# An encoder block on one core: values products of a head moved back, selection rounds spread, and one weight of a short pair summed on chip

## The chip, the cores and the metric

The kernel runs on one core of a Trainium2 chip. A core has TensorE (matmuls, PE in the profile; its weight loads are PEld), VectorE (DVE), ScalarE (ACT), GpSimd (POOL) and SyncE (SP, which here only issues DMAs). Each engine works through its own queue in order; semaphores tie the queues together. The metric is the device time of one execution in microseconds: 1687.0 us, the median of three runs (1686.08 to 1688.25).

## The reference, cut to what matters

One layer of a streaming encoder on 512 frames of width 2048, all in float32:

```
h = rmsnorm(x)
aq, ak, av, az, iq, ik, iw, rq, rk, rv, rz, ga, gb = split(h @ w_in)
index  = sum over 16 heads of relu(iq . ik) * iw           # which keys a query may use
sel    = the top 128 keys of each query, within its chunks
a_out  = softmax(aq . ak * scale + bias, over sel) @ av * silu(az)      # 8 heads of 128
b_out  = groupnorm(retention(rope(rq), rope(rk), rv)) * silu(rz)        # 8 heads of 128
merged = sigmoid(ga) * (a_out @ w_a_out) + sigmoid(gb) * (b_out @ w_b_out)
r = x + merged @ w_o
y = rmsnorm(r + (p @ w_ple) * sigmoid(r @ w_ple_gate))
```

Nearly all of the arithmetic is matrix products of 512 frames with weights that are read once. Three places matter here: the product of a head's probabilities with its values (`@ av`), the selection of the top keys, and the product `b_out @ w_b_out`.

## The kernel before

**Weights in two parts.** TensorE multiplies a weight block as a high part (float32r) and a low part, the rest. A *unit* is one weight block of up to eight 128x128 tiles. For each unit SyncE loads a raw tile (`wraw`, line 150), ScalarE writes the high part `wh` (line 176), VectorE subtracts it from the raw tile and so writes the low part `wl` (line 183). Raw tiles have 7 slots, `wh` and `wl` 3 each. Splitting runs `AHEAD` = 3 units before use (`reach`), loading `LOADS` = 5 units before that (`load_reach`).

**Pairs.** Two output blocks are computed together from seven products instead of eight (`gemm_pair`). The seven weights are sums of the four blocks b11, b12, b21, b22 (`block_pair`): the first is b12 + b22, the second b11, then b21 and b22; the fifth is the first + b11, the sixth the fifth + b21, and the seventh b11 + b12. In the order of the code's tuples the raw tile `t` is used for the first, fifth and sixth, and `w11` for the second and the seventh. b12 + b22 is made by a DMA that accumulates onto the loaded tile (`add_block`, line 137, issued by GpSimd). So are the fifth weight (b11 onto `t`, once the first weight has been split) and the seventh (b12 onto `w11`, once the second has been split). Only b21 is added by VectorE (line 185), as that tile is on chip anyway. The sums of the frames that go with the seven products are made earlier. In a pair, the products go to four PSUM banks p, v, q, r; after some of them ScalarE copies a bank (`pv`, `e`, line 279) and VectorE takes differences (`e_t`, line 283). The bank p is used by the second, fifth and seventh product, and the next of these on it waits for the copy.

**Short pairs.** Most pairs have blocks of eight tiles. The four pairs of `b_out @ w_b_out` (`project_two`, for m = 6, 8, 10, 12) have blocks of four. Two raw tiles, two `wh` or two `wl` of such units share one slot (`shared`). While such units are near, loads run up to `HALF_LOADS` = 14 units ahead, and the accumulation that makes b12 + b22 is issued 16 steps after its load. The differences of a short pair are added by GpSimd (line 1276), two by two: after the third and the sixth product one addition each, after the seventh two.

**Steps.** The order of all side work is written out in steps. `step()` is called after every two matmuls of a pair (56 steps in a pair, 28 in a short one) or every three of a plain product; `later(n, f)` puts f into the queues n steps on. What is put there stands in each engine's queue at that place and runs when the engine reaches it and its semaphores allow.

**Heads.** Attention head h is spread over three pairs (`attention_head`): its query and key product is the pair itself; logits, softmax and transposes of the probabilities (`ps_pt`) run beside the next pair; ScalarE's high part `pth` and VectorE's low part `ptl` (line 1143) at the turn to the pair after; then the values products (`outs`, line 1157), at 69, 69, 73, 73 steps after the head's own pair, which is at steps 13 and 17 of a pair of 56. The product of the third matmul uses the low part of the second block, the sixth that of the third. The gate (line 1170) runs on GpSimd at 77, the store at 92. The logits of the next head come at steps 20, 22, 24 and 26 of the same pair. PSUM has 8 banks, of which the pair holds four.

**Selection.** The top keys are found in 16 rounds for each of three tiles of queries, each a `MAX8` and a `MATCH_REPLACE8` on VectorE (lines 767, 768). Rounds are background work: `step` takes one from a list when the step number is a multiple of the current rate. In the four `rz` pairs and the three `az` pairs that follow (from 774.8 to 923.9 us) the rate is `BG_RATES[5]` = 9. The list has to be empty after them; the mask is then stored, and added to the bias tile of each head by a DMA 8 steps before the end of its own pair (line 1072).

Of the kernel before, what the change touches and what calls it, by code (L numbers as in the profile page):

```python
# [34 lines left out]
def block_kernel(tc, xT, pT, posb, posq, w_in, w_v, w_k, w_a, w_b, w_o, w_ple, w_gate,  # L35
                 w_gt, w_pt, fgb, tab, xg, cst, dec, out, out_a, out_b):
    nc = tc.nc
    pe, dve, act, pool, sp = nc.tensor, nc.vector, nc.scalar, nc.gpsimd, nc.sync

    with contextlib.ExitStack() as ctx:  # L40
# [10 lines left out]
        def U(name, dt=F32):  # L51
            return up.tile([128, L], dt, name=name, tag="u")

        def B(name, dt=F32):
            return bp.tile([128, 1280], dt, name=name, tag="b")

        def P(name):
            return pp.tile([128, L], F32, name=name, tag="p")
# [11 lines left out]
        raw_tiles = {}  # L70
# [5 lines left out]
        def raw(src, k0, nk, cols, plus=None):  # L76
            raws.append((src, k0, nk, cols, plus))
            return len(raws) - 1
# [9 lines left out]
        def block_pair(s1, s2, nk=8):  # L88

            b11, b12, b21, b22 = (s1, 0), (s2, 0), (s1, nk), (s2, nk)
            first = len(units)
            t = raw(*b12, nk, 128, b22)
            w11, w21, w22 = (raw(*b, nk, 128) for b in (b11, b21, b22))
            for r, plus in ((t, b11), (w11, b12), (w21, None), (w22, None), (t, w21), (t, None), (w11, None)):
                units.append((r, plus, nk, 128))
            if nk < 8:
                half_raws.update((t, w11, w21, w22))
                half_units.update(range(first, first + 7))  # L100
            return list(range(first, first + 7))

        half_raws, half_units = set(), set()
        open_tiles = {}

        def shared(kind, dt, tag, bufs=None):
            t = open_tiles.pop(kind, None)
            if t is not None:
                return t[:, 4:8, :]
            more = {} if bufs is None else {"bufs": bufs}  # L110
            t = open_tiles[kind] = wp.tile([128, 8, 128], dt, name=tag, tag=tag, **more)
            return t[:, 0:4, :]

        def load_reach(i):
            n = i + AHEAD + LOADS
            if any(i + d in half_units for d in range(AHEAD)):
                n = max(n, min(i + HALF_LOADS, max(half_units) + 3))
            return n
# [13 lines left out]
        def view(t, nk, cols):  # L132
            return t.rearrange("p a c -> p (a c)")[:, 0:nk * cols].rearrange("p (a c) -> p a c", c=cols)

        def add_block(r, b):
            src, k0 = b
            pool.dma_start(out=raw_tiles[r], in_=src[:, k0:k0 + raws[r][2], :], accum_op=OP.add)  # L137

        def load_to(n):
            need = max((u[0] for u in units[:n]), default=-1) + 1  # L140
            while state["raw"] < need:
                i = state["raw"]
                src, k0, nk, cols, plus = raws[i]
                if nk * cols <= L and i < 4:
                    t = U("wraw4").rearrange("p (a c) -> p a c", c=128)
                elif i in half_raws:
                    t = shared("raw", F32, "wraw", RAW_BUFS)
                else:
                    t = wp.tile([128, 8, 128], F32, name="wraw", tag="wraw", bufs=RAW_BUFS)
                sp.dma_start(view(t, nk, cols), src[:, k0:k0 + nk, :])  # L150
                raw_tiles[i] = t
                if plus is not None:
                    later(16 if i in half_raws else 0, lambda i=i, plus=plus: add_block(i, plus))
                state["raw"] += 1

        def split_to(n):
            while state["split"] < min(n, len(units)):
                i = state["split"]
                load_to(i + 1)
                r, plus, nk, cols = units[i]  # L160
                if r in unfinished:
                    unfinished[r]()
                raw = view(raw_tiles[r], nk, cols)
                if i in half_units:
                    h, l = (shared(n, F32R, n) for n in ("wh", "wl"))
                elif i in in_raws:
                    t = wp.tile([128, 2, 512], F32R, name="whl", tag="wraw", bufs=RAW_BUFS)
                    h, l = t[:, 0:1], t[:, 1:2]
                elif nk * cols == L:
                    h, l = (U(n, F32R).rearrange("p (a c) -> p a c", c=cols) for n in ("wh4", "wl4"))  # L170
                else:
                    h, l = (view(wp.tile([128, 8, 128], F32R, name=n, tag=n), nk, cols) for n in ("wh", "wl"))
                if i == 0:
                    dve.tensor_copy(h, raw)  # L174
                else:
                    act.activation(h, raw, AF.Copy)  # L176

                def rest(i=i, r=r, plus=plus, l=l, raw=raw, h=h, nk=nk, cols=cols):
                    if i in finished:
                        return  # L180
                    finished.add(i)
                    unfinished.pop(r)
                    dve.tensor_sub(l, raw, h.bitcast(F32))  # L183
                    if isinstance(plus, int):
                        dve.tensor_add(raw, raw, view(raw_tiles[plus], nk, cols))  # L185
                    elif plus is not None:
                        add_block(r, plus)

                unfinished[r] = rest
                later(1 if i else 0, rest)  # L190
                loaded[i] = (h, l)
                state["split"] += 1
# [7 lines left out]
        def later(n, f):  # L200
            if n <= 0:
                return f()
            tick[1] += 1
            heapq.heappush(soon, (tick[0] + n, tick[1], f))
# [234 lines left out]
        for k in range(KT):  # L439
# [7 lines left out]
            elif k < 10:  # L447
                t = U("xk")
                sp.dma_start(t, xT[:, k, :])
                xs.append(t)  # L450
            elif k % 2 == 0:
                t = B("xk2")
# [277 lines left out]
        def values_store(c0, pss):  # L730
            for t, ps in enumerate(pss):
                n = ps.shape[1]
                v = U("rv")[:, 0:n]
                act.activation(v, ps, AF.Copy, scale=R["nat"][:, t:t + 1])
                act.dma_start(rd[t, :, c0:c0 + n], v)
# [8 lines left out]
        for n, f in ((50, f_pos), (54, lambda: f_table(0)), (59, lambda: f_table(1))):  # L744
            later(n, f)
        state["rate"] = BG_RATES[0]
        values_store(0, values(u_rv[0], 512, late=2))
        state["rate"] = BG_RATES[1]
        pss = values(u_rv[1], 296)
        f_keys0(pss)  # L750
        todo.extend([None] * 4 + [f_keys1] + [None] * 10 + [f_keys2] + N3 * 4 + [f_keys3] + N3 * 2)
        state["rate"] = BG_RATES[2]
        ix = [iq_split(gemm(u_iq[m], hparts, "ps_iq", slice(128, L))) for m in range(IQ_PLAIN)]
# [7 lines left out]

        state["rate"] = BG_RATES[1]

# [224 lines left out]
        assert not bg, len(bg)  # L988
        state["rate"] = BG_RATES[3]
        for m in range(IQ_PLAIN):  # L990
# [37 lines left out]
        for kind, n, u in pairs:  # L1028
# [9 lines left out]
            else:  # L1038
# [4 lines left out]
                elif n == G_FIRST:  # L1043
                    state["rate"] = BG_RATES[4]
                gate_pair(u, to(d[m:m + 2], AF.Sigmoid))
# [16 lines left out]
        def attention_head(h):  # L1062
# [85 lines left out]
            def outs(n):  # L1148
                if n == 0:
                    E["po"] = P("ps_o")  # L1150
                po = E["po"]
                for i in range(3 * n, min(3 * n + 3, len(seq))):
                    a, b, j = seq[i]
                    if j == NT - 1:
                        pe.matmul(po[:, 384:], E["v"][0][:, tok(3)].bitcast(F32), E["p3"][:, 0:128], start=False, stop=False)
                    else:
                        pe.matmul(po[:, 128 * j:], E["v"][a][:, tok(j)], E["p"][b][:, JOFF[j]:JOFF[j] + L - 128 * j],
                                  start=(i == 0), stop=(i == len(seq) - 1))
                if n == 3:
                    E["oT"] = U("oT")  # L1160
                    act.activation(E["oT"], po, AF.Copy)
# [13 lines left out]
            steps = [(-30, loads), (-8, mask), (30, values_load)]  # L1175
# [2 lines left out]
            steps += [(54, lambda i=i: turn(i)) for i in range(3)]  # L1178
            steps += [(n, lambda i=i: high(i)) for i, n in enumerate((56, 56, 58))]
            steps += [(n, lambda i=i: low(i)) for i, n in enumerate((58, 58, 60))]  # L1180
            steps += [(n, lambda i=i: outs(i)) for i, n in enumerate((69, 69, 73, 73))]
            steps += [(48, z_load), (77, gate), (92, store)]
            return done, steps

        for n in range(Z_FIRST):
# [2 lines left out]
        for h in range(NH):  # L1188
            done, steps = attention_head(h)
# [110 lines left out]
        for m in PAIRED:  # L1300
            t = B("sm")
# [97 lines left out]
        for m in range(MF):  # L1399
            i = u_p[m // 4][0]  # L1400
# [12 lines left out]
            if m < Y_APART or m >= Y_APART + 2:  # L1413
                t = U("pw")
            else:
                if m == Y_APART:
                    ypair[m // 2] = B("y2")
                t = ypair[m // 2][:, L * (m % 2):L * (m % 2) + L]
# [44 lines left out]
        for n in range(MF // 2):  # L1463
            t = B("go")
            outs = t[:, 0:512], t[:, 512:1024]
# [156 lines left out]
AHEAD = 3  # L1622
LOADS = 5
BG_RATE = 4
BG_RATES = (3, 3, 4, 10, 8, 9)
IQ_PLAIN = 2
G_FIRST = 2
X_STAY = 3
# [3 lines left out]
ROUNDS_FIRST = 0  # L1632
PAIR_STEPS = 56
B_PAIRS = 6
HALF_LOADS = 14
Z_FIRST = 3
ROUND_GAP = 11
STORE_LAG = 16
# [97 lines left out]
```

## Time and profile before

| | |
|---|---|
| runs, median (lowest to highest) | 1687.0 us (1686.08 to 1688.25) |
| profiled execution | 1688.58 us |
| its span, first to last instruction | 1686.8 us |
| granted TensorE clock, mean | 0.995 |
| TensorE matmul busy | 1654.5 us, 98% |
| VectorE busy | 1420.1 us, 84% |
| ScalarE busy | 963.2 us, 57% |
| GpSimd busy | 352.7 us, 21% |
| mean DMA rate | 227 GB/s |

How to read it: a row of the timeline gives start, length, engine, source line and operation, output and inputs; in brackets the idle time of the engine before it and what ended that. A row of the waits says who waited for whom, the total in us, how often, and the longest. A row of the stage windows gives the window, its length, the busy time of PE, PEld, DVE, ACT and POOL, the granted clock as a share of the full one, the DMA share and GB/s. The ends of matmuls are modelled; their starts are not.

### The profile page before, as it was taken

What the parts mean: (1) busy time and instruction counts of PE and PEld (TensorE: products, weight loads), DVE (VectorE), ACT (ScalarE), POOL (GpSimd) and SP (SyncE); (2) the same over time, 40 slices, a digit from 0 to 9 for tenths busy, and PEclk for the clock granted to TensorE, in tenths of its full rate; (3) what the DMA queues carried; (4) which work ended last, traced back from release to release, by engine and by line L of the source; (5) the groups of instructions that cost most, each with busy time, mean ns of one, the idle gap of its engine ahead of it and who ended that gap; (6) DMA issues with size and microseconds to landing.
All of it is one profiled execution on the core that took longest, in us unless ns stands there. A gap on an engine that the chain in (4) does not pass through costs nothing.

```text
span 1686.8 us, 26584 instructions
## 1 busy us (share of the span) xinstructions
PE 1654.5 (98%) x9632; PEld 1457.4 (86%) x9632; DVE 1420.1 (84%) x2257; ACT 963.2 (57%) x1501; POOL 352.7 (21%) x355
## 2 busy tenths in 40 slices
PE   9999999999999999999999999999899999999998
PEld 7999998888888888888888877878788888888897
DVE  8789887888889889889997777678788888899895
ACT  6557666555555555555545656557443454487673
POOL 3011111111111111111554112124330033311211
PEclk9999999999999999999999999999999999999999
DMA  8779888887888888877879998875987699999873
GB/s 305 255 238 253 206 209 198 207 205 198 216 208 212 210 206 214 221 199 209 245 197 232 255 239 206 235 178 207 276 301 222 161 251 287 260 322 238 214 243 125
DMA packets 144163, 382.19 MB, mean 227 GB/s; under 512 B 15648, under 2 KB 30112, under 8 KB 144032
## 3 DMA queue, kind: packets, MB, share of 16 engines
q1 hardware_dynamic: 106528, 261.20, 44.5%
q0 software_dynamic: 29872, 106.44, 35.2%
q10 hardware_dynamic: 7632, 12.85, 2.2%
q8 instruction: 76, 1.25, 0.3%
q14 instruction: 55, 0.45, 0.1%
HBM read 331.28 MB, written 49.15 MB: 226 GB/s over the span
## 4 chain that ended last, share of the span: by engine, by line
PE 79%; DVE 8%; ACT 4%; DMA 3%; issue 3%; POOL 2%; POOLq 0%; SPq 0%; ACTq 0%; DVEq 0%
PE ps_p L319 25%; PE ps_v L319 16%; PE ps_q L319 9%; PE ps_r L319 9%; PE ps_vn L720 6%; DVE wl L183 4%; DMA wraw<-w_b 2%; PE ps_w L239 2%; PE ps_w L238 2%; PE ps_w L240 2%; ACT wh L176 1%; DVE e_t L283 1%; DVE isc L768 1%; DVE m L767 1%; ACT bm L1110 1%
## 5 line engine op out<-in xcount | busy, mean ns | idle before, releaser
L183 DVE TENSOR_TENSOR wl<-wraw,wh 128x1024 fp32r<-128x1024 f32 (+1 forms) x521 | 630.4, 1215 | 164.3 <-ACT wh L176 156.1
L176 ACT ACTIVATE wh<-wraw 128x1024 fp32r<-128x1024 f32 (+2 forms) x520 | 523.7, 1017 | 307.8 <-DVE wraw L185 148.5
L137 POOL DMA_DIRECT2D wraw<-w_in x141 | 124.7, 919 | 747.7 <-DVE wl L183 209.4
L279 ACT ACTIVATE e<-ps_p 128x512 f32<-128x512 f32 (+1 forms) x195 | 115.2, 591 | 166.5 <-PE ps_p L319 161.1
L319 PE MATMUL ps_p<-hs,wh 128*128 128x512 f32 (+1 forms) x752 | 189.7, 391 | 0.0
L319 PEld LDWEIGHTS ps_p<-hs,wh 128*128 128x128 f32 x752 | 134.0, 189 | 23.5 <-issue 1.2
L319 PE MATMUL ps_p<-hs,wl 128*128 128x256 f32 (+1 forms) x752 | 106.3, 283 | 4.9 <-DVE wl L183 4.3
L319 PEld LDWEIGHTS ps_p<-hs,wl 128*128 128x128 f32 x752 | 96.8, 191 | 6.8 <-ACT wh L176 3.8
L319 PE MATMUL ps_p<-ha,wh 128*128 128x512 f32 (+1 forms) x376 | 98.2, 399 | 0.0
L319 PE MATMUL ps_r<-hs,wh 128*128 128x512 f32 (+1 forms) x376 | 96.5, 391 | 0.0
L319 PE MATMUL ps_q<-ha,wh 128*128 128x512 f32 (+1 forms) x376 | 94.5, 390 | 0.0
L319 PE MATMUL ps_v<-ha,wh 128*128 128x512 f32 (+1 forms) x376 | 92.9, 388 | 0.0
L319 PE MATMUL ps_v<-hs,wh 128*128 128x512 f32 (+1 forms) x376 | 92.2, 386 | 0.0
L185 DVE TENSOR_TENSOR wraw<-wraw 128x1024 f32<-128x1024 f32 (+1 forms) x65 | 82.4, 1267 | 2.2
L319 PEld LDWEIGHTS ps_q<-ha,wh 128*128 128x128 f32 x376 | 71.2, 190 | 14.3
L319 PEld LDWEIGHTS ps_v<-hs,wh 128*128 128x128 f32 x376 | 70.2, 188 | 13.9
L319 PEld LDWEIGHTS ps_v<-ha,wh 128*128 128x128 f32 x376 | 69.6, 188 | 13.2
L319 PEld LDWEIGHTS ps_p<-ha,wh 128*128 128x128 f32 x376 | 68.3, 193 | 11.5 <-ACT wh L176 0.4
L319 PEld LDWEIGHTS ps_r<-hs,wh 128*128 128x128 f32 x376 | 67.2, 189 | 10.8
L283 DVE TENSOR_TENSOR e_t<-ps_p,pv 128x512 f32<-128x512 f32 (+1 forms) x59 | 40.2, 681 | 30.9 <-ACT e L279 30.8
L720 PE MATMUL ps_vn<-wh,hh 128*128 128x296 f32 (+1 forms) x192 | 63.3, 335 | 0.3 <-DVE wh L174 0.3
L720 PE MATMUL ps_vn<-wl,hh 128*128 128x296 f32 (+1 forms) x192 | 62.2, 329 | 0.0
(452 smaller groups left out, 3587.7 us busy)
## 6 DMA issues: line engine op xcount, KB each, us to landing
wraw<-w_in SPq DMA_DIRECT2D x192, 512.0 KB, 5.0
wraw<-w_in POOLq DMA_DIRECT2D x141, 512.0 KB, 7.8
wraw<-w_o SPq DMA_DIRECT2D x32, 512.0 KB, 7.0
wraw<-w_o POOLq DMA_DIRECT2D x24, 512.0 KB, 7.5
wraw<-w_gate SPq DMA_DIRECT2D x24, 512.0 KB, 6.1
wraw<-w_gate POOLq DMA_DIRECT2D x18, 512.0 KB, 6.9
wraw<-w_a SPq DMA_DIRECT2D x16, 512.0 KB, 5.5
rl<-rr SPq DMA_DIRECT2D x24, 256.0 KB, 5.9
```

Source lines behind the costliest of these rows:

```text
L137: pool.dma_start(out=raw_tiles[r], in_=src[:, k0:k0 + raws[r][2], :], accum_op=OP.add)
L176: act.activation(h, raw, AF.Copy)
L183: dve.tensor_sub(l, raw, h.bitcast(F32))
L185: dve.tensor_add(raw, raw, view(raw_tiles[plus], nk, cols))
L238: pe.matmul(o, h[:, k, w], a, start=(s == order[0]), stop=False)
L239: pe.matmul(o, h[:, k, w], b, start=False, stop=False)
L240: pe.matmul(o, l[:, k, w], a, start=False, stop=(s == order[-1]))
L279: act.activation(E[n], src, AF.Copy)
L283: f(t, x, y)
L319: pe.matmul(to, w[:, k], x, start=(n < 4 and part == parts[0] and k == order[0]), stop=(part == parts[1] and k == order[-1]), skip_group_c ...
L720: pe.matmul(pss[t], x[:, tok(t)], w[:, k], start=(s == 0 and n < NT * len(run) and x is a and w is h), stop=(s == KT - 1 and x is b))
L767: dve.max(m8, a)
```

## The change

Four edits. In a short pair the fifth weight is made on chip: GpSimd adds the raw tile of the second weight (b11, plain) to `t`, where a DMA had accumulated b11 from HBM; so that `w11` stays plain, the seventh weight has a raw tile of its own, loaded as b11 with b12 accumulated 16 steps later. A short pair then has five raw tiles, not four. The negative number in the tuple says that GpSimd adds. With it `HALF_LOADS` goes from 14 to 11. The values products of a head move from 69, 69, 73, 73 to 75, 75, 80, 80 steps, the gate from 77 to 84 and the store from 92 to 98. The rate of the rounds in the `rz` and `az` pairs goes from 9 to 11.

```
@@ block_pair
-            for r, plus in ((t, b11), (w11, b12), (w21, None), (w22, None), (t, w21), (t, None), (w11, None)):
+            if nk == 8:
+                w1, p0, p1 = w11, b11, b12
+            else:
+                w1, p0, p1 = raw(*b11, nk, 128, b12), -w11, None
+                half_raws.update((t, w11, w21, w22, w1))
+            for r, plus in ((t, p0), (w11, p1), (w21, None), (w22, None), (t, w21), (t, None), (w1, None)):
                 units.append((r, plus, nk, 128))
             if nk < 8:
-                half_raws.update((t, w11, w21, w22))
                 half_units.update(range(first, first + 7))
@@ split_to, rest
                     if isinstance(plus, int):
-                        dve.tensor_add(raw, raw, view(raw_tiles[plus], nk, cols))
+                        (dve if plus > 0 else pool).tensor_add(raw, raw, view(raw_tiles[abs(plus)], nk, cols))
@@ attention_head
-            steps += [(n, lambda i=i: outs(i)) for i, n in enumerate((69, 69, 73, 73))]
-            steps += [(48, z_load), (77, gate), (92, store)]
+            steps += [(n, lambda i=i: outs(i)) for i, n in enumerate((75, 75, 80, 80))]
+            steps += [(48, z_load), (84, gate), (98, store)]
@@ constants
-BG_RATES = (3, 3, 4, 10, 8, 9)
+BG_RATES = (3, 3, 4, 10, 8, 11)
-HALF_LOADS = 14
+HALF_LOADS = 11
```

## The prediction

> **What bounds the kernel.** I read the page's head first, then the table of waits, then stage windows of one pair each, then the order in time where TensorE waits.
>
> ```profile
> span 1686.8 us, 26584 instructions
> PE 1654.5 (98%) x9632; PEld 1457.4 (86%) x9632; DVE 1420.1 (84%) x2257; ACT 963.2 (57%) x1501; POOL 352.7 (21%) x355
> ```
> ```profile
> PE ps_o L1157 <- DVE ptl L1143: 11.0, 14, 1.5
> ...
> PE ps_p L319 <- ACT e L279: 6.3, 4, 2.6
> ...
> PE ps_p L319 <- DVE wl L183: 4.3, 7, 0.7
> ```
> Columns of the second: who waited for whom, us in total, times, longest. TensorE is at work 98% of the span, so a change pays only where TensorE waits. Of its 32 us without work (1686.8 less 1654.5), 21.6 are these three waits, and each belongs to one edit: the values products, the short pairs, the selection rounds. Bare matmul time comes from a pair in a calm place:
>
> ```profile
> 820.10 1.98 PE L319 MATMUL ps_v<-hs,wh 128*128 128x512 f32 x8
> 821.92 1.11 PE L319 MATMUL ps_v<-hs,wl 128*128 128x256 f32 x8
> 822.87 1.12 PE L319 MATMUL ps_p<-ha,wl 128*128 128x256 f32 x8
> ```
> Starts are 1.82/8 = 0.23 us apart for 512 columns and 0.95/8 = 0.12 for 256. A full pair is 7 x 8 x 0.35 = 19.5 us, a short one half of that, 9.7.
>
> **Values products, six steps later.** Seven pairs carry a head's values products beside a pair. Two of them, and the pair before with none:
>
> ```profile
> 943.40:966.37 22.97, 22.79 (x134) 19.90 (x133) 17.13 (x29) 15.48 (x26) 3.46 (x4) 1.00 0.94 253
> 966.37:992.85 26.48, 24.81 (x146) 21.51 (x145) 19.68 (x33) 16.10 (x31) 5.34 (x5) 1.00 0.87 229
> 992.85:1020.86 28.01, 26.35 (x145) 22.69 (x144) 19.88 (x33) 16.49 (x32) 5.15 (x5) 0.94 0.84 212
> ...
> 1047.11:1075.13 28.02, 26.36 (x145) 22.76 (x144) 19.88 (x33) 16.53 (x32) 4.85 (x5) 0.94 0.81 215
> 1101.39:1129.38 27.99, 26.34 (x145) 22.75 (x144) 19.14 (x33) 16.50 (x32) 5.82 (x5) 0.94 0.72 177
> ```
> Columns: length, busy PE, PEld, DVE, ACT, POOL, granted clock, DMA share, GB/s. Inside such pairs:
>
> ```profile
> 970.58 0.57 PE L1157 MATMUL ps_o<-pth,av 128*128 128x512 f32 x2
> 971.41 1.15 DVE L1143 TENSOR_TENSOR ptl<-ps_pt,pth 128x512 fp32r<-128x512 f32 x2
> 972.62 0.44 PE L1157 MATMUL ps_o<-ptl,av 128*128 128x384 f32 x1 [1.47 <-DVE ptl L1143]
> 973.08 0.41 DVE L1143 TENSOR_TENSOR ptl<-ps_pt,pth 128x256 fp32r<-128x256 f32 x1
> 973.55 0.39 PE L1157 MATMUL ps_o<-ptl,av 128*128 128x256 f32 x1 [0.20 <-DVE ptl L1143]
> ...
> 1000.26 2.76 PE L319 MATMUL ps_p<-ha,wh 128*128 128x512 f32 x6
> 1002.82 0.99 PE L319 MATMUL ps_q<-ha,wh 128*128 128x512 f32 x2
> ```
> The third and sixth products need the low part, which VectorE ends at 972.56 and 973.49. A modelled matmul ends some 0.16 us after the next could start, so the 14 waits cost 11.0 + 14 x 0.16 = 13.2 us. After some of them the clock drops: from 1000.26 six matmuls start 0.43 apart, not 0.23. The three pairs at 0.94 last 1.5 longer than the one at 1.00: 4.5 us. Together 17.7.
>
> Steps 14 to 19 hold twelve 512-column matmuls, 12 x 0.23 = 2.7 us. The third product would come at 971.0 + 2.7 = 973.7, 1.1 us after its low part; the sixth, three matmuls on, 0.6 us after. No order on VectorE changes, and it has room: 19.7 busy in a pair that would shrink to about 24.5. What is late next: banks are handed out in the order in which they come free, and the products' bank now comes free after the second logits tile and not before the first, so that the fourth logits tile takes the bank of the first and must wait until VectorE has read it; and the transposes at the pair's end have less time behind the softmax. I leave 2.2 for both, 0.3 a pair: **-15.5**. Bounds: the 11.0 alone and all 17.7. The gate on GpSimd and the store on SyncE move back seven and six steps; behind them stand weight accumulations and loads that are asked for eight units ahead, so they cost nothing; if one came late it would be a wait like those of the short pairs.
>
> The clock rows deserve a second look. [...] The rows, slow right behind a 1.5 us wait and nowhere in the calm pairs, speak for the wait as the cause.
>
> **Selection rounds, every eleventh step.**
>
> ```profile
> 798.39:820.10 21.71, 20.42 (x117) 17.76 (x116) 20.82 (x42) 11.92 (x15) 11.45 (x12) 1.00 0.84 224
> 820.10:841.39 21.29, 19.97 (x113) 17.32 (x112) 21.05 (x33) 10.18 (x13) 12.49 (x13) 1.00 0.92 253
> 841.39:861.82 20.43, 19.78 (x114) 17.30 (x112) 20.16 (x32) 10.18 (x13) 11.44 (x11) 1.00 0.82 218
> 861.82:884.29 22.47, 20.23 (x113) 17.24 (x112) 22.23 (x31) 10.18 (x13) 11.11 (x12) 1.00 0.76 188
> 884.29:904.41 20.12, 19.72 (x113) 17.26 (x112) 19.14 (x27) 10.53 (x13) 9.52 (x9) 1.00 0.94 233
> 904.41:923.90 19.49, 19.49 (x113) 17.22 (x112) 12.34 (x12) 10.29 (x13) 7.36 (x9) 1.00 0.87 236
> ```
> ```profile
> L767 DVE MAX8 m<-isc 128x8 f32<-128x384 f32 (+2 forms) x6 | 3.3, 551 | 0.0
> L768 DVE MATCH_REPLACE8 isc<-m,isc 128x384 f32<-128x384 f32 (+2 forms) x6 | 3.3, 542 | 0.0
> ```
> Four of these pairs are VectorE's: it is busy 98% of them, and they run 1 to 3 us over 19.5. A round is 0.55 + 0.54 = 1.1 us. A pair has 56 steps, so it carries 5.1 rounds for 6.2, 1.2 us less. Gains, no more than the excess: 1.2, 1.2, 0.9, 1.2, or 4.5. The displaced rounds fall on the last two pairs: the fifth (19.14 of 20.12 busy) has no room and loses about 0.7, the sixth (12.34 of 19.49) takes its share for 0.3. **-3.5**, bounds +1 and -6. Some 35 turns of 11 steps are 385 of the 392 that the seven pairs have; the mask, stored then, is read 48 steps into the next pair, 17 us on, and no landing quoted here is above 10.
>
> **Short pairs: fifth weight on GpSimd, loads 11 units ahead instead of 14.**
>
> ```profile
> 1190.49:1238.47 47.98, 41.69 (x225) 35.72 (x224) 35.39 (x48) 23.32 (x41) 20.89 (x22) 0.96 0.97 299
> ```
> ```profile
> 1199.02 0.88 POOL L137 DMA_DIRECT2D wraw<-w_b  x1 [10.64 <-DVE wl L183]
> 1201.11 1.07 PE L319 MATMUL ps_v<-bs,wh 128*128 128x512 f32 x4
> 1201.91 1.26 POOL L1276 TENSOR_TENSOR bo<-e_t 128x256 f32<-128x256 f32 x1
> 1205.62 0.63 ACT L176 ACTIVATE wh<-wraw 128x512 fp32r<-128x512 f32 x1 [5.57 <-DMA wraw<-w_b]
> 1207.80 1.15 ACT L176 ACTIVATE wh<-wraw 128x512 fp32r<-128x512 f32 x2 [0.57 <-DVE wraw L185]
> 1208.85 0.58 ACT L279 ACTIVATE e<-ps_p 128x512 f32<-128x512 f32 x1
> 1209.48 0.74 PE L319 MATMUL ps_p<-bs,wl 128*128 128x256 f32 x4 [2.64 <-ACT e L279]
> ```
> Four short pairs take 48.0 us for 38.9: 9.1 lost. The second shows how: the accumulation into its fifth weight, issued at 1199.02, lands 6.6 us later; ScalarE stands before that weight; the copy `e` that TensorE's fifth product needs is queued behind that. Due at 1201.1 + 4 x 1.39 = 1206.7, the product starts at 1209.5.
>
> GpSimd's add does away with this wait: for this size a tensor instruction of GpSimd takes 1.3 to 1.9 us, so it is done by 1201 where the DMA landed at 1205.6.
>
> ```profile
> L1052 POOL TENSOR_TENSOR go<-go,y x8: 1302/1446/1866, 805.8 to 870.3; 128x512 f32<-128x512 f32 x8
> ...
> DMA to landing us min/median/max: 4.3/7.0/10.0
> ```
> (The second row is of the twelve accumulations into w_b's tiles.) As many DMAs move as before, five loads and two accumulations for four and three. But their places in GpSimd's queue change. In steps from the start of the first short pair, four to a product, its additions stand at 12, 24 and, two, at 28. An accumulation stands 16 behind its load, and loads are now asked for 11 units ahead. So the second pair's seventh weight is loaded at 12, accumulated at 28, behind the addition at 24 (the row at 1201.91), and wanted by ScalarE at 32. The third pair's first weight is loaded at 16 (before: 4), accumulated at 32 (20), behind the two additions, and wanted at 40; the fourth's at 44, 60, 64. In the second and the fourth pair the seventh weight stands before copy `e` of the second product (the x2 row at 1207.80, then 1208.85).
>
> The second pair then: accumulation issued at 1201.9 + 1.3 = 1203.2, landing 6.6 later at 1209.8, weight and copy 1.1, TensorE at 1210.9, 4.2 late for 2.8 now. The third pair's first weight: 1203.2 + 0.9 to issue + 2.0 for two additions, landing at 1212.7, two weights and copy `e` of the fifth product 1.7, 1214.4, for a seventh product due at 1210.9 + 2.8: 0.7 late. The third pair: its own fifth weight comes 0.5 late, as its add waits for that first weight; then the fourth's first weight, issued about 4 us after the third's start (copy, two differences, two additions), landing at 10.6, three weights and a copy later 12.5, for a seventh product due at 8.3: 4.2. The fourth: its seventh weight's accumulation stands behind GpSimd's own add, which follows that first weight, and behind two additions: issued at 15.4, landed at 22.0, copy at 23.1, for a product due at 20.0: 3.1. The first pair keeps the 0.8 that are left of the 9.1 for it. Sum 13.5; with half clock after two of the waits, 1.4 each at the 0.2 us a matmul seen above, 16.3 for 9.1: **+7**. Bounds: -9.1, if every accumulation comes in time, and, with five landings of 10.0 for 6.6, +24. I take the landing seen in place, as it is near the median.
>
> Against the add itself speaks this: it could hold back VectorE's subtractions. In this stage VectorE has room:
>
> ```profile
> DVE wl L183 <- ACT wh L176: 12.3, 9, 3.9
> ```
> It stands 12.3 us before ScalarE here, more than four adds of 1.9, so I count nothing; without that cover it is up to 7.6. [...]
>
> **Sum.** -15.5 - 3.5 + 7 = -12. The profiled execution is 1688.6 (span 1686.8 and 1.8 around it), 1.6 above the runs' median of 1687.0; off the median: **1675**.
>
> **Rivals.**
> - A, the short pairs gain: accumulations are issued early enough (GpSimd runs ahead where nothing holds it). For: GpSimd stood idle 10.64 us before 1199.02, so its queue has room. Against: the additions in its queue follow TensorE. Then 1687 - 19 - 8 = 1660.
> - B, slower: the late accumulations of the short pairs land like the slowest. Place: ScalarE before the seventh and first weights. Price 3.4 us in each of five: 1675 + 17 = 1692. It decides from a landing of about 9 us. For: DMA share 0.97 in this stage. Against: the median of 7.0.
> - C, the edit of the values products does not do what it says: VectorE's low parts slip as much as the products, or the reused logits bank brings the wait back. Then 1675 + 15.5 = 1690.5. Against: a quarter of VectorE idle in these pairs.
> - D, the slow clock in the head pairs is not the waits' doing and stays: 1675 + 4.5 = 1679.5. For: it comes in every second pair, though each has the waits. Against: it begins right behind a wait, and no pair without one has it.
>
> **Chances.** Forecast 0.58, A 0.24, B 0.06, C 0.07, D 0.05. The forecast's own range is 1668 to 1682. Low end 1658: A with all 17.7; high end 1684: the values products at 11.0, rounds -1, short pairs at 9. A measurement of this kernel tells about 0.2% (3.4 us) from no change. Faster: forecast, A and D less their tails, 0.86; same 0.05 and slower 0.09 from B, C and the forecast's tail.
>
> **What would show it.** The table of waits loses L1157 on L1143, and the pairs from 966 on last 24.3 to 24.8 at clock 1.00; if 26 or more, the first step is wrong. The pairs between 798 and 884 last 20 to 21, the next carries five rounds. The short pairs take about 55 us, with ScalarE's waits for DMA moved to seventh and first weights and TensorE waiting at seventh products too; 39 to 42 us there means A, over 65 B.

## The result, and the profile after

The changed kernel takes **1677.89 us** (median of four runs, 1676.29 to 1679.89) beside 1687.62 us for the kernel before, run in turn with it (1686.08 to 1691.16): a ratio of 0.994, with a 95% interval of 0.9921 to 0.9959. It is faster, by 9.7 us where 12 were forecast. The profiled execution is 1676.29 us, the lowest of these four and 12.3 less than the profiled one of before; so the terms read from the two profiles add up to more than the medians differ by. In the changed kernel lines named before are four further on (L319 is L323, L137 is L141, L1157 is L1161, L1276 is L1280).

From the table of waits, what TensorE still waits for:

```profile
PE ps_p L323 <- ACT e L283: 16.7, 5, 6.7
PE ps_p L323 <- DVE wl L187: 1.3, 3, 0.5
```

Of the three waits of before, that of the values products (11.0 us) is gone, that behind VectorE's low parts has shrunk from 4.3 to 1.3, and that behind ScalarE's copies has grown from 6.3 to 16.7. So two edits gained and one lost. The stage windows of the pairs with rounds, of two head pairs, and of the four short pairs with their total (length, busy PE, PEld, DVE, ACT, POOL, granted clock, DMA share, GB/s):

```profile
774.53:797.57 23.04, 23.04 (x144) 20.68 (x143) 22.66 (x40) 11.16 (x15) 5.14 (x5) 1.00 0.81 227
797.57:817.50 19.93, 19.93 (x118) 17.65 (x116) 19.72 (x38) 12.16 (x15) 11.74 (x12) 1.00 0.93 255
817.50:836.99 19.49, 19.49 (x113) 17.22 (x112) 18.68 (x28) 10.41 (x13) 10.57 (x12) 1.00 0.95 261
836.99:856.62 19.63, 19.63 (x113) 17.27 (x112) 18.78 (x29) 10.52 (x13) 10.07 (x11) 1.00 0.88 233
856.62:878.14 21.52, 20.24 (x113) 17.24 (x112) 20.70 (x28) 10.40 (x13) 9.69 (x12) 1.00 0.79 200
878.14:897.64 19.50, 19.50 (x114) 17.22 (x112) 19.30 (x28) 10.30 (x13) 7.64 (x8) 1.00 0.83 205
897.64:918.40 20.76, 20.21 (x114) 17.24 (x112) 20.37 (x27) 10.29 (x13) 8.29 (x9) 1.00 0.90 238
...
960.87:985.10 24.23, 24.23 (x145) 21.61 (x144) 19.18 (x34) 16.36 (x32) 4.82 (x5) 1.00 0.93 249
1082.03:1106.27 24.24, 24.24 (x146) 21.61 (x144) 18.97 (x33) 16.13 (x32) 4.83 (x5) 1.00 0.84 203
...
1165.38:1176.56 11.18, 10.02 (x57) 8.64 (x56) 6.52 (x10) 6.18 (x11) 2.62 (x3) 1.00 1.01 306
1176.56:1192.36 15.80, 11.61 (x57) 9.80 (x56) 11.63 (x16) 5.74 (x10) 7.18 (x8) 0.89 0.66 200
1192.36:1207.32 14.96, 10.26 (x58) 8.71 (x56) 9.75 (x12) 6.66 (x12) 6.11 (x7) 1.00 0.92 285
1207.32:1226.26 18.94, 12.26 (x57) 10.45 (x56) 13.00 (x17) 5.44 (x8) 7.21 (x9) 0.82 0.68 209
1165.38:1226.26 60.88, 44.16 (x225) 37.60 (x224) 40.91 (x52) 24.01 (x41) 23.12 (x25) 0.92 0.79 243
```

Set beside the windows of before, each of the three terms is read off alone:

| Term | Forecast | Measured | How |
|---|---|---|---|
| values products | -15.5 (-11.0 to -17.7) | **-19.6** | six pairs of 26.25 to 28.02 now at 24.23 or 24.24: -17.6; the stretch behind them, 61.11 to 59.11: -2.0 |
| selection rounds | -3.5 (+1 to -6) | **-5.2** | seven pairs, 149.1 to 143.9 |
| short pairs | +7 (-9.1 to +24) | **+12.9** | 47.98 to 60.88 |
| sum | -12.0 | **-11.9** | profiled executions: -12.3 |

The sum fits by luck: three errors of -4.1, -1.7 and +5.9 cancel. It is no proof of the terms; the experiments take them one by one.

The short pairs are where a reader learns most. The second pair, in order of time on GpSimd, ScalarE and TensorE (brackets: the idle time before, and what ended it):

```profile
1177.94 1.12 POOL L1280 TENSOR_TENSOR bo<-e_t 128x256 f32<-128x256 f32 x1 [1.23 <-DVE e_t L287]
1179.01 0.86 POOL L141 DMA_DIRECT2D wraw<-w_b  x1
...
1185.32 0.63 ACT L180 ACTIVATE wh<-wraw 128x512 fp32r<-128x512 f32 x1 [4.25 <-DMA wraw<-w_b]
1185.85 0.58 ACT L283 ACTIVATE e<-ps_p 128x512 f32<-128x512 f32 x1
...
1186.49 0.75 PE L323 MATMUL ps_p<-bs,wl 128*128 128x256 f32 x4 [4.19 <-ACT e L283]
```

GpSimd may issue the accumulation of the seventh weight only behind its addition, which waits for VectorE's difference `e_t` of TensorE's results. ScalarE stands before that weight for 4.25 us, and the copy that TensorE's fifth product needs is queued behind it. The third and the fourth pair:

```profile
1194.71 1.73 POOL L1280 TENSOR_TENSOR bo<-e_t 128x256 f32<-128x256 f32 x2
1196.09 1.19 POOL L141 DMA_DIRECT2D wraw<-w_b  x1
...
1209.92 1.12 POOL L1280 TENSOR_TENSOR bo<-e_t 128x256 f32<-128x256 f32 x1 [2.43 <-DVE e_t L287]
1210.98 0.88 POOL L141 DMA_DIRECT2D wraw<-w_b  x1
```
```profile
1197.76 0.63 ACT L180 ACTIVATE wh<-wraw 128x512 fp32r<-128x512 f32 x1 [4.09 <-DVE wraw L189]
...
1203.62 1.67 ACT L180 ACTIVATE wh<-wraw 128x512 fp32r<-128x512 f32 x3 [2.17 <-DMA wraw<-w_b]
...
1218.57 0.63 ACT L180 ACTIVATE wh<-wraw 128x512 fp32r<-128x512 f32 x1 [5.53 <-DMA wraw<-w_b]
```
```profile
1199.42 0.74 PE L323 MATMUL ps_p<-bs,wl 128*128 128x256 f32 x4 [1.32 <-ACT e L283]
...
1205.83 0.74 PE L323 MATMUL ps_p<-bs,wl 128*128 128x256 f32 x4 [3.38 <-ACT e L283]
...
1219.73 1.22 PE L323 MATMUL ps_p<-bs,wl 128*128 128x256 f32 x4 [6.68 <-ACT e L283]
1220.75 1.91 PE L323 MATMUL ps_p<-bs,wh 128*128 128x512 f32 x4
```

The same chain twice more, before the products at 1205.83 and 1219.73 (the row at 1197.76 waits for VectorE's add and for no DMA). In the fourth pair the accumulation leaves GpSimd at 1210.98 and lands 7.6 us later, and TensorE stands for 6.7 us before the fifth product. The next 512-column matmuls then start 1.71/4 = 0.43 us apart (1220.75 to 1222.46), at a granted clock of 0.50 (1217.80 to 1224.63).

### The profile page after: what moved, and what is told of

It is laid out like the page before. It is cut to its first block, busy times and chain, and to the rows that moved or that the text cites. A ratio compares the mean times of both kernels' runs of the same rounds, so it can differ in the third digit from the quotient of the medians.

```text
span 1674.5 us, 26595 instructions
## 1 busy us (share of the span) xinstructions
PE 1646.6 (98%) x9632; PEld 1455.5 (87%) x9632; DVE 1420.8 (85%) x2257; ACT 964.2 (58%) x1501; POOL 349.7 (21%) x355
## 5 line engine op out<-in xcount | busy, mean ns | idle before, releaser
L141 POOL DMA_DIRECT2D wraw<-w_in x141 | 125.4, 924 | 735.1 <-DVE wl L187 216.4
L323 PE MATMUL ps_p<-hs,wh 128*128 128x512 f32 (+1 forms) x752 | 189.7, 391 | 0.0
L323 PEld LDWEIGHTS ps_p<-hs,wh 128*128 128x128 f32 x752 | 134.0, 189 | 23.4 <-issue 1.2
L323 PE MATMUL ps_p<-hs,wl 128*128 128x256 f32 (+1 forms) x752 | 105.9, 283 | 1.3 <-DVE wl L187 1.3
L323 PEld LDWEIGHTS ps_p<-hs,wl 128*128 128x128 f32 x752 | 96.9, 191 | 2.4 <-ACT wh L180 1.2
L323 PE MATMUL ps_r<-hs,wh 128*128 128x512 f32 (+1 forms) x376 | 96.5, 391 | 0.0
L323 PE MATMUL ps_p<-ha,wh 128*128 128x512 f32 (+1 forms) x376 | 94.1, 390 | 0.0
L323 PE MATMUL ps_q<-ha,wh 128*128 128x512 f32 (+1 forms) x376 | 93.2, 386 | 0.0
L323 PE MATMUL ps_v<-ha,wh 128*128 128x512 f32 (+1 forms) x376 | 92.9, 388 | 0.0
L323 PE MATMUL ps_v<-hs,wh 128*128 128x512 f32 (+1 forms) x376 | 92.2, 386 | 0.0
L323 PEld LDWEIGHTS ps_v<-hs,wh 128*128 128x128 f32 x376 | 70.2, 188 | 13.9
L323 PEld LDWEIGHTS ps_q<-ha,wh 128*128 128x128 f32 x376 | 69.8, 188 | 13.2
L323 PEld LDWEIGHTS ps_v<-ha,wh 128*128 128x128 f32 x376 | 69.6, 188 | 13.2
L189 DVE TENSOR_TENSOR wraw<-wraw 128x1024 f32<-128x1024 f32 (+1 forms) x65 | 78.5, 1207 | 2.2
L323 PEld LDWEIGHTS ps_p<-ha,wh 128*128 128x128 f32 x376 | 67.2, 189 | 11.7 <-ACT wh L180 0.4
L323 PEld LDWEIGHTS ps_r<-hs,wh 128*128 128x128 f32 x376 | 67.2, 189 | 10.8
L724 PE MATMUL ps_vn<-wh,hl 128*128 128x296 f32 (+1 forms) x192 | 62.1, 329 | 0.0
```

What stands on the lines that cost most here:

```text
L189: (dve if plus > 0 else pool).tensor_add(raw, raw, view(raw_tiles[abs(plus)], nk, cols))
L323: pe.matmul(to, w[:, k], x, start=(n < 4 and part == parts[0] and k == order[0]), stop=(part == parts[1] and k == order[-1]), skip_group_c ...
L724: pe.matmul(pss[t], x[:, tok(t)], w[:, k], start=(s == 0 and n < NT * len(run) and x is a and w is h), stop=(s == KT - 1 and x is b))
```

## Experiments

A part alone comes first (1 to 3), then the short pairs taken apart (4 to 7, 9, 12), then their repair (8, 9), then the clock (10, 11). Times are medians; ratios are to the kernel before, run in the same series.

**1. The values products alone** (`e1_heads`): before, with

```
-  steps += [(n, lambda i=i: outs(i)) for i, n in enumerate((69, 69, 73, 73))]
-  steps += [(48, z_load), (77, gate), (92, store)]
+  steps += [(n, lambda i=i: outs(i)) for i, n in enumerate((75, 75, 80, 80))]
+  steps += [(48, z_load), (84, gate), (98, store)]
```

> The kernel before with the values products, the gate and the store moved back alone. Theory (the three edits act in separate stages and add up): the seven pairs with values products last 24.2 us at clock 1.00 instead of 26.3 to 28.0, the rest is as before, short pairs 48.0 us; the time is 19.6 us less than before, 1668. Rival (the gain needs the thinner selection rounds ahead of it, or is handed back in the short pairs): less than 15 us gained, or short pairs over 52 us.

Measured 1668.53 us, ratio 0.9885 (0.987 to 0.9899). The first of the six pairs, and the short pairs, which this edit leaves alone:

```profile
965.97:990.21 24.24, 24.24 (x146) 21.61 (x145) 19.15 (x34) 16.37 (x32) 4.80 (x5) 1.00 0.96 249
...
1170.49:1219.16 48.67, 41.41 (x226) 35.66 (x224) 36.44 (x49) 23.22 (x41) 22.44 (x23) 0.96 0.94 291
```

This one edit gains 19.4 us. All six pairs last 24.23 or 24.24 us, and TensorE is busy for the whole of it: no wait has taken the place of the old one.

**2. The rate alone** (`e2_rate`): before, with

```
-BG_RATES = (3, 3, 4, 10, 8, 9)
+BG_RATES = (3, 3, 4, 10, 8, 11)
```

> The kernel before with the selection rounds on every eleventh step alone. Theory: the seven pairs from 774.8 us on are 5.2 us shorter in all, the pairs with values products keep 26.3 to 28.0 us, short pairs 48.0; the time is 5 us less, 1682. Rival (VectorE's lighter load there does not reach TensorE, the stage was shorter for another reason): the seven pairs are within 1 us of before, time within 2 us of 1687.

Measured 1681.97 us, ratio 0.9967 (0.9956 to 0.9979), 5.9 us less. The seven pairs last 23.04, 19.92, 19.50, 19.63, 21.53, 19.49 and 20.75, within 0.02 of the changed kernel's. Something else moved too: the head pairs keep their waits here, but in this execution the slow clock is in one of six, and not in three.

```profile
1040.58:1068.59 28.01, 26.35 (x146) 22.74 (x144) 19.16 (x33) 16.50 (x32) 5.91 (x5) 0.94 0.83 213
```

The six pairs take 160.1 us for 163.0. That this 2.9 is the edit's doing is not shown: it compares one execution of each kernel, and the mean granted clock of the executions runs from 0.993 to 0.997 in the kernel before and in this one alike. The three parts alone add up to -19.4 - 5.9 + 13.3 = -12.0. The whole gains 9.7 by the medians, with an interval of 6.9 to 13.3 that holds the 12.0, so these times show no effect of one edit on another.

**3. The short pairs alone** (`e3_short`): before, with the edit of `block_pair`, GpSimd's add and `HALF_LOADS = 11`.

> The kernel before with the short pairs' edit alone (fifth weight added by GpSimd, seventh weight's own tile, loads 11 units ahead). Theory: the four short pairs last 60.9 us instead of 48.0, all else as before; 13 us more, 1700. Rival (the short pairs are slow because the stages ahead of them became faster): short pairs within 3 us of 48, time near 1687.

Measured 1701.15 us, ratio 1.0077 (1.0062 to 1.0092): 13.3 us slower.

```profile
1190.62:1251.24 60.62, 44.28 (x225) 37.87 (x224) 40.63 (x52) 23.93 (x41) 22.98 (x24) 0.89 0.79 243
```

The stage is 12.6 longer than before, as in the full change: nothing of the loss comes from the other two edits.

**4. All but the short pairs** (`e4_no_short`): the changed kernel with `block_pair`, the add and `HALF_LOADS = 14` as before.

> The changed kernel with the short pairs' edit undone (weights and loads ahead as before; values products and rounds as changed). Theory: short pairs 48.0 us again, 13 us less than the changed kernel, 25 less than before: 1663 to 1665. Rival (accumulating DMAs are late there whatever makes the weights, as TensorE now comes sooner): short pairs over 54 us, time over 1670.

Measured 1664.47 us, ratio 0.986 (0.9846 to 0.9875); the stage takes 47.27 us.

Undoing this one edit makes the changed kernel 13.4 us faster by the medians (13.6 in the stage).

**5 and 6. Which half of the edit: the weights or the reach?** `e5_old_weights_11` is experiment 4 with only the reach changed; `e6_new_weights_14` is the changed kernel with only the reach put back:

```
-HALF_LOADS = 14      # 5: from experiment 4
+HALF_LOADS = 11
-HALF_LOADS = 11      # 6: from the changed kernel
+HALF_LOADS = 14
```

> The changed kernel with the short pairs' weights made as before (fifth and seventh by an accumulating DMA onto a used tile), and loads 11 units ahead as in the change. It lies beside the run with the short pairs' edit undone (1664.5, short pairs 47.3 us). Theory (the shorter reach is what costs: it puts an accumulation later in GpSimd's queue, behind additions that follow TensorE): short pairs 55 to 60 us, time 1672 to 1677. Rival (the new weights cost, by the add on GpSimd or by the seventh weight's new accumulation, the reach does not): short pairs 47 to 49, time 1664 to 1666.

> The changed kernel with loads 14 units ahead again. Theory (the reach costs): the accumulations of seventh and next first weight go in front of the pair's last additions, short pairs 60.9 down to 45 to 50 us, time 1662 to 1667. Rival (the new weights cost): 58 us or more, time over 1674.

Measured 1668.83 us (0.9891, 0.9876 to 0.9905) and 1662.26 us (0.9849, 0.9833 to 0.9865). The stage of each:

```profile
1165.55:1217.86 52.31, 44.61 (x225) 38.09 (x224) 35.16 (x48) 23.22 (x41) 20.96 (x22) 0.90 0.90 274
```
```profile
1165.43:1213.27 47.84, 41.97 (x226) 35.82 (x224) 37.67 (x49) 23.80 (x41) 23.55 (x23) 0.96 0.91 289
```

With the old weights a reach of 11 for 14 costs 52.31 - 47.27 = 5.0 us; with the new ones 60.88 - 47.84 = 13.0. The new weights at the old reach cost 0.6, less than the stage differs between kernels that have it as before (47.0 to 48.8). So the new weights alone are neither the gain that they could have been nor the loss, the shorter reach alone costs 5.0, and the two together 13.6: most of the loss needs both. TensorE's waits for the copies `e` say the same: 5.7 us in experiment 4, 7.6 in 5, 5.8 in 6 and 16.7 in the changed kernel; the rest of the 5.0 comes with the slower clock (0.90 for 0.96). Experiment 6 fell into its range; experiment 5 missed both of its ranges, as the reach alone had been expected to cost some 8 us or more. By the code, the new seventh weight too is accumulated a fixed number of steps behind its load, and not when the second weight has been split, so that a shorter reach delays it as well.

**7. A longer reach** (`e7_new_weights_16`): the changed kernel with `HALF_LOADS = 16`.

> The changed kernel with loads 16 units ahead. Theory: all accumulations stand a whole product or more ahead of the additions they were behind; only the first pair's loss of about 1 us is left, short pairs 40 to 43 us, time 1657 to 1660, faster than with the short pairs' edit undone (1664.5). Rival (seven raw tiles are too few for this reach, loads then wait for a free tile and with them everything on SyncE): short pairs no better than 48, time 1665 or more.

Measured 1660.96 us, ratio 0.9843 (0.9828 to 0.9857); the stage takes 45.45 us. That is the shortest stage seen, but more than expected: TensorE still loses 3.1 us at the third pair's fifth product. The timeline there, on all engines:

```profile
1184.97 2.62 DVE L187 TENSOR_TENSOR wl<-wraw,wh 128x512 fp32r<-128x512 f32 x1
1185.61 1.42 POOL L189 TENSOR_TENSOR wraw<-wraw 128x512 f32<-128x512 f32 x1
...
1192.69 1.09 DVE L189 TENSOR_TENSOR wraw<-wraw 128x512 f32<-128x512 f32 x1
...
1193.82 0.63 ACT L180 ACTIVATE wh<-wraw 128x512 fp32r<-128x512 f32 x1 [5.71 <-DVE wraw L189]
...
1194.83 0.59 ACT L283 ACTIVATE e<-ps_p 128x512 f32<-128x512 f32 x1
...
1195.47 0.74 PE L323 MATMUL ps_p<-bs,wl 128*128 128x256 f32 x4 [2.95 <-ACT e L283]
```

No DMA is late here. ScalarE stands 5.71 us before the sixth weight. VectorE, which adds it, works without a gap from 1184.97 on and comes to this add last, and the copies are queued behind it: the same place in ScalarE's queue, held by another engine.

**8. The accumulations moved forward, the reach left at 11** (`e8_lag4`): the changed kernel with

```
-  later(16 if i in half_raws else 0, lambda i=i, plus=plus: add_block(i, plus))
+  later(4 if i in half_raws else 0, lambda i=i, plus=plus: add_block(i, plus))
```

> The changed kernel, loads still 11 units ahead, each accumulation of a short pair's weight 4 steps behind its load instead of 16. Theory (not the time of the load but the place of the accumulation in GpSimd's queue decides): short pairs 44 to 49 us, time 1661 to 1666. Rival (the loads themselves come too late): the accumulation now waits in GpSimd's queue for its load and holds up what stands behind, short pairs 58 us or more, time over 1674.

Measured 1664.10 us, ratio 0.9861 (0.9846 to 0.9876); the stage:

```profile
1165.72:1213.71 47.99, 41.52 (x225) 35.76 (x224) 38.19 (x49) 23.88 (x41) 24.35 (x23) 0.96 0.92 292
```

This run settles the cause. Loads, weights, adds and the number of DMAs are those of the changed kernel; only the place of the accumulations in GpSimd's queue is another, and 12.9 us of the stage go.

**9. Both** (`e9_16_lag4`): the changed kernel with reach 16 and the accumulations 4 steps behind their loads.

> The changed kernel with both repairs: weight loads 16 units ahead and each accumulation 4 steps behind its load. Theory (what reach 16 left is ScalarE's copies behind the sixth weight, which waits for VectorE's add, and no accumulation): no gain over reach 16 alone, short pairs 44 to 46 us, 1660 to 1662. Rival (some accumulations of reach 16 were still late): short pairs 41 to 43, 1656 to 1659.

Measured 1661.53 us, ratio 0.985 (0.9834 to 0.9867), the stage 45.86 us. Once the accumulations are early enough, making them earlier gives nothing more. 7 and 9, which the measurement does not tell apart, are the fastest versions seen, some 26 us below the kernel before.

**12. Reach 16 with the old weights** (`e12_old_weights_16`): experiment 4 with `HALF_LOADS = 16`.

> The kernel with the first two edits, the weights of the short pairs as before (fifth and seventh accumulated by DMA) and loads 16 units ahead. Does the fifth weight on chip gain anything, or the reach alone? Theory (the fifth weight's accumulation is issued when the first weight has been split, which the reach does not bring forward, so its landing still holds ScalarE in most pairs): short pairs 46 to 48 us, 1663 to 1665. Rival (the reach alone did what the run with the new weights and reach 16 showed): 45 to 46, 1660 to 1662.

Measured 1663.16 us, ratio 0.9859 (0.9843 to 0.9876); the stage takes 47.11 us.

The reach alone gives 0.2 us (47.27 to 47.11). With the new weights the stage is 1.7 shorter, 45.45, but not by fewer waits: TensorE waits 5.4 us for the copies here and 5.5 in experiment 7. The difference goes with the clock, 0.96 here and 1.00 there, and the intervals of the two whole kernels overlap. So no run shows that the fifth weight on chip gains anything.

**10 and 11. What brings the slow clock?** The kernel before, with the third product's wait made shorter and longer:

```
-  enumerate((69, 69, 73, 73))
+  enumerate((71, 71, 75, 75))     # 10
+  enumerate((66, 66, 70, 70))     # 11
```

> The kernel before with the values products of a head two steps later (71, 71, 75, 75) in place of six: the third product's wait, 1.6 us in the kernel before, should shrink by some 0.9 to about 0.7. [...]

> The kernel before with the values products of a head three steps earlier (66, 66, 70, 70): the third product's wait should grow by some 1.4 to about 3.0. Theory (length and place together): head pairs of 27.9 where the clock stays and 29.3 where it drops, and it drops in five or six of six, 1700 to 1703. [...]

One run of each: 1676.55 and 1691.69 us. In 10 the wait is 0.3 to 0.6 us, the pairs last 25.25 to 25.54, and none is slow. In 11 the waits are 2.4 us, 1 us longer than before, and yet only the first of the six pairs is slow, fewer than in the kernel before. The rows of its first pair, which lasts 28.79 us, and of its second, 27.31 us:

```profile
972.42 0.44 PE L1157 MATMUL ps_o<-ptl,av 128*128 128x384 f32 x1 [2.42 <-DVE ptl L1143]
...
974.59 1.91 PE L319 MATMUL ps_p<-ha,wh 128*128 128x512 f32 x4
```
```profile
1001.17 0.44 PE L1157 MATMUL ps_o<-ptl,av 128*128 128x384 f32 x1 [2.38 <-DVE ptl L1143]
...
1002.80 1.08 PE L319 MATMUL ps_p<-ha,wh 128*128 128x512 f32 x4
```

Four matmuls take 1.91 us in the one and 1.08 in the other, behind waits of the same length. My theory for 11, that longer waits bring the drop in five or six of six pairs, falls: something beside the length of a wait decides. What it is, no run shows; the last section has what was measured.

## Why the prediction was right or wrong, step by step

**What bounds the kernel** held: the three waits of TensorE that were named are the places where time moved; all the rest together changed by 0.4 us.

**Values products: right in mechanism, too small in size.** Forecast -15.5, measured -19.6, and 19.4 by the edit alone; this is outside the bound of 17.7. The slack came as worked out. The low part ends at 965.91 + 1.15 = 967.06, and the third product, no longer waiting, starts at 968.20: 1.1 after it, as forecast.

```profile
965.91 1.15 DVE L1147 TENSOR_TENSOR ptl<-ps_pt,pth 128x512 fp32r<-128x512 f32 x2
...
968.20 0.34 PE L1161 MATMUL ps_o<-ptl,av 128*128 128x384 f32 x1
```

Three sizes were off. The step "I leave 2.2 for both" priced two new waits, the reused logits bank and the transposes; neither shows, in pairs where TensorE is busy for all of 24.23 us. "A modelled matmul ends some 0.16 us after the next could start" priced a pair's waits at 1.89 us (13.2/7); by the starts of the matmuls it is 2.0 (26.25 to 24.23, and the last stretch). And "the three pairs at 0.94 last 1.5 longer" compared 28.01 with 26.48, when the other undisturbed pairs last 26.25: it is 1.76. So 7 x 2.0 + 3 x 1.76 = 19.3, and the 0.2 by which one pair of 26.48 stands above the others. A gain should be measured against the bare length that a view gives, here a pair without a wait, and not by adding up idle times. That the gate and the store cost nothing by moving held.

**Selection rounds: right in sign, -5.2 for -3.5.** Three steps were off. The first of the seven pairs was left out of the sum, and became 0.5 shorter. "Gains, no more than the excess: 1.2, 1.2, 0.9, 1.2" gave 1.8, 1.8, 0.8 and 1.0. Each gain stayed within the pair's excess; the 1.2 was wrong, an average for what the edit takes out of a pair. By the two instructions of the rounds VectorE lost 1.6, 1.6, 0.9 and 1.4 us of work in these pairs. And "the fifth has no room and loses about 0.7" was wrong in sign: it became 0.6 shorter (20.12 to 19.50), with no less work on VectorE (19.30 us for 19.14). The likely reason is that a VectorE that is 98% busy hands its lateness on, and that this pair had carried the debt of the ones ahead: it has 1.8 us more of rounds now, and 1.6 less of other work. The rows fit this, but no run tests it. Only the last took the displaced rounds: +1.3 where 0.3 was forecast, with VectorE at 20.37 of 20.76. The mask came in time.

**Short pairs: right in mechanism and place, +12.9 for +7.** Lost against the bare 38.9 us, forecast and measured by the starts of the matmuls:

| Step | Forecast | Measured |
|---|---|---|
| first pair | 0.8 | 1.3 |
| second, fifth product (seventh weight) | 4.2 | 4.4 |
| second, seventh product | 0.7 | 0 |
| third, fifth product | 0.5 | 1.5 |
| third, seventh product (the fourth's first weight) | 4.2 | 3.5 |
| fourth (its seventh weight) | 3.1 | 6.8 |
| slow clock | 2.8 | 4.0 |
| sum | 16.3 | 21.5, and 0.5 in small ones |

The two large steps of the middle came within 0.7. The 0.7 that did not come is a landing of 4.2 us (issued at 1182.84) for the 6.6 that was used everywhere. The step that failed is the fourth pair's "issued at 15.4". It put the accumulation 1 us after the start of that pair, when it stands behind the addition that the row at 1209.92 shows, 2.6 us into the pair; the same accumulation of the second pair had been put 2.1 after that start, and the row there showed it. It left 3.7 after (1210.98 less 1207.32), which is 2.7 late, and landed after 7.6 and not 6.6: 3.7 in all, the difference between 3.1 and 6.8. That addition waited for VectorE's difference, which starts at 1209.17: VectorE works without a gap from 1204.29 on, after ScalarE's wait for the fourth pair's first weight (the row at 1203.62), and comes to the difference only then. By these rows one late accumulation delays the next; the sum had followed GpSimd's add behind that weight, but not VectorE's queue. The third pair's 1.5 is not the wait that was named, for GpSimd's add: ScalarE waits 4.09 us for VectorE's add (the row at 1197.76), a wait that the kernel before had too, 2.03 us long. The landings themselves were about as assumed (six accumulations in the stage):

```profile
DMA to landing us min/median/max: 4.1/7.1/8.3
```

"GpSimd's add does away with this wait" was true, and no gain. In experiment 6 no DMA makes the fifth weight and the stage is no shorter: ScalarE waits 9.3 us there for VectorE's adds of the sixth weights, where it was 4.7 in the kernel before.

**The add against VectorE.** Counted at nothing for its cover; nearly right. The 28 subtractions of this size took 830 ns each before and 873 after, 1.2 us in all:

```profile
L187 DVE TENSOR_TENSOR wl<-wraw,wh 128x512 fp32r<-128x512 f32 x28 | 23.8, 873 | 18.8 <-ACT wh L180 18.8
```
```profile
L183 DVE TENSOR_TENSOR wl<-wraw,wh 128x512 fp32r<-128x512 f32 x28 | 22.6, 830 | 12.3 <-ACT wh L176 12.3
```

Single rows beside GpSimd's adds are long: in experiment 7 the subtraction beside an addition and the add of GpSimd (1184.53 to 1187.03) took 2.62 us, where another takes 0.69 (at 1194.48). But the new adds changed the total little, and the kernel before has such rows too: two subtractions from 1199.13 on, beside an addition of GpSimd, took 2.10 us. That the one instruction held the other back is not shown.

**The rivals.** A (short pairs gain) fell for this change; GpSimd did not run ahead. Its time of 1660 is what the change reaches with a reach of 16 (1660.96), but not by A's sum: the short pairs take 45.45 us there, not 39 to 42. B fell: no landing was above 8.3. C fell. D fell as a forecast, all head pairs being at 1.00; but experiments 2 and 11 show that what stood for it, slow phases in some pairs and not in others with the same waits, is real (the last section has the times).

## What to carry to other kernels

In the second short pair of the changed kernel an accumulating DMA left GpSimd only behind the addition ahead of it in the queue (at 1179.01; the addition took 1.12 us from 1177.94 on). When a load distance is shortened, walk each issue through its queue and ask what it now stands behind, above all instructions that wait for another engine. A constant lag of a few steps can then be worth more than the distance (experiment 8: 12.9 us from one number). Measure a promised gain against the length of a stage without the wait, and count the work that an edit takes out of each stage instead of an average over all of them.

## What the runs showed of the hardware

The clock. Behind a wait of TensorE of 1.5 us the granted clock dropped to half for 3.4 us (512-column matmuls 0.43 us apart for 0.23), in three of six pairs in the kernel before and one of six in experiment 2 with the same waits; behind waits of 2.4 us in one of six (experiment 11); behind the changed kernel's wait of 4.19 us it dropped, within that of 6.68 us too, and behind that of 3.38 us it did not (the third short pair is at 1.00). Behind waits of 0.6 and less (experiment 10) it never did in these pairs. So the length of a wait alone does not decide.

The granted clock by the profiles, between start-up and the end of the matmuls. In the kernel before it is 0.50 from 1000.19 to 1003.60 us, from 1054.80 to 1058.21, from 1109.41 to 1112.83 and from 1222.05 to 1225.47; in the changed kernel from 1187.08 to 1190.49 and from 1217.80 to 1224.63. Five of these six phases last 3.41 us and one 6.83. Their starts lie 54.61, 54.61 and 112.64 us apart in the one profile and 30.72 in the other: by these numbers 16, 16, 33 and 9 times the length of one phase. In the 3.41 us ahead of each phase TensorE is busy for 1.75, 1.75, 1.75 and 1.58 us in the kernel before, and for 0.59 and 0.00 in the changed one. But around the changed kernel's wait of 3.38 us it is busy for 1.72 us from 1200.73 to 1204.15 and for 1.73 from there to 1207.56, less than the 1.75 ahead of three of those phases, and the clock stays at 1.00. So these times do not show what decides beside the length of a wait.

What follows for measuring: with waits of the same length, slow phases came in three of six pairs in one execution and in one of six in another (the kernel before and experiment 2). A slow phase in a head pair costs 1.76 us, 28.01 for 26.25, so a difference of that size between single executions should be looked up in the clock first.
